# Moving 24 gathered rows and ten expert columns ahead of the gate stage's end, with scores one unit later

## The chip, the cores and the metric

One core of one Trainium2 chip runs the kernel. The metric is the device time of one execution in microseconds, lower is better. The kernel before took 2283.4 us (median of three runs, 2283.37 to 2287.0).

## The reference, cut to what matters

Two transformer blocks over 512 tokens of width 1024, in fp32. The change lies in the last layer, a retrieval of experts: each token scores 16 x 128 sub-keys, keeps 16 experts for each of 8 heads out of 16384, and adds up their outputs.

```python
def block(xb):
    q = (xb @ w_query).reshape(T, PEER_HEADS, 2, PEER_HALF)
    s = jnp.einsum('thpk,hpnk->thpn', q, sub_keys).astype(jnp.float32)
    top_s, top_i = lax.top_k(s, PEER_TOPK)
    ...
    best_s, best_pos = lax.top_k(cand_s.reshape(T, PEER_HEADS, PEER_TOPK * PEER_TOPK), PEER_TOPK)
    idx = jnp.take_along_axis(..., best_pos, axis=-1)
    gate = jax.nn.softmax(best_s, axis=-1)
    u = expert_u[idx]
    v = expert_v[idx]
    act = jax.nn.gelu(jnp.einsum('td,thkd->thk', xb, u).astype(jnp.float32), approximate=False)
    return jnp.einsum('thk,thkd->td', (gate * act).astype(xb.dtype), v)
```

## The kernel before

Tokens are four tiles of 128. The expert layer, `peer`, treats them in two ways.

**Tile 0 by rows.** `gather` (L1065) reads, for each of 128 expert slots, one row of u and later one row of v for every token, by an indirect DMA that the POOL queue issues (L1074, 512 KB each, 256 in all, four buffers `grow`). VectorE reduces a u row with the token's activations (L1077) or adds a v row into `acc0` (L1079). In the program these rows stand in `experts_out`, about two behind each column.

**Tiles 1 to 3 densely.** The 16384 experts are 128 columns of 128. For a column, `expert_in` (L1056) makes the hidden activations of the 384 tokens: `unit` (L189) loads 512 KB of weights into one of three `raw` buffers, ScalarE writes the high part `whi` (L200), VectorE or POOL the low part `wlo` (L201) into one of eight buffers of the pool `wsp`, TensorE does 24 matmuls of 384 tokens (L206 to L208), ScalarE the Gelu (L1062). An even column is made early and spilled to `actD` (64 of them, NSPILL); odd columns are made fresh in the last stage.

`peer` runs in four stages, whose instructions a planner orders on each engine by program order and modelled readiness; every engine then works its queue in order.
- **Scores** (`route`, L1095 to L1108): 16 units of the query; after each unit's projection ScalarE copies q, TensorE multiplies it with the sub-keys (L1103), and VectorE takes the top 16 (`top16`).
- **Top 16 of the pairs** (L1109 to L1158): VectorE alone, with TensorE on expert columns beside it.
- **Gates** (`gates_dense`, L1180): 96 blocks of four tokens. A block needs a tile A (the first index's one-hot times the gate) and a tile B (the second index's one-hot), then small matmuls (L1216) and a copy (L1218). Tile A is built by POOL in blocks 2 and 6 of eight (L1199), by ScalarE in 0 and 4 (L1203, L1204), by VectorE otherwise (L1210); B by VectorE (L1213, and L1206 where ScalarE built A). There are six buffers each. The blocks leave through `gst` to `gD` in memory. 24 steps of four blocks each.
- **Products with v** (`experts_out`, L1226): for each column, `parts` takes the activations (spilled, or fresh), loads the gates `gt` for eight columns at a time (L1247), multiplies (L1257), splits (L1261, L1262), loads v, and 18 matmuls of 512 follow (`prod`). Three columns (1, 3, 5) are made ahead of the first product.

`pace` (L1039) says how many columns are traced beside each stage: 3 and 2 beside the scores, 45 beside the top 16, 14 beside the gates. Their `wlo` is VectorE's work in the 45 and POOL's in the others.

## Time and profile before

| | |
|---|---|
| median of three runs | 2283.4 us |
| the profiled execution | 2284.21 us |
| its span | 2282.4 us |
| TensorE busy, share of the span | 96% |
| VectorE, ScalarE, POOL busy | 74%, 40%, 30% |
| mean granted TensorE clock | 0.986 |

The profile lists what each engine did and when, from the span's start. A busy share is an average over the whole span; the stages differ. In the views below a number such as `x118` counts instructions; a part in brackets or behind the bar says how long the engine sat idle and what ended that. `PEclk` is the share of full clock that TensorE was granted: 1.00 is 2.4 GHz, 0.50 is 1.2 GHz. The stages of `peer` lie at about 990 to 1140 us (scores), 1140 to 1319 (top 16), 1313 to 1462 (gates) and 1462 to 2282 (products).

### The profile page before, as it was taken

What the parts mean: (1) busy time and instruction counts of PE and PEld (TensorE: products, weight loads), DVE (VectorE), ACT (ScalarE), POOL (GpSimd) and SP (SyncE); (2) the same over time, 40 slices, a digit from 0 to 9 for tenths busy, and PEclk for the clock granted to TensorE, in tenths of its full rate; (3) what the DMA queues carried; (4) which work ended last, traced back from release to release, by engine and by line L of the source; (5) the groups of instructions that cost most, each with busy time, mean ns of one, the idle gap of its engine ahead of it and who ended that gap; (6) DMA issues with size and microseconds to landing.
All of it is one profiled execution on the core that took longest, in us unless ns stands there. A gap on an engine that the chain in (4) does not pass through costs nothing. (4 is left out here: it accounts for less than half of the span.)

```text
span 2282.4 us, 32112 instructions
## 1 busy us (share of the span) xinstructions
PE 2201.8 (96%) x11849; PEld 1952.1 (86%) x11849; DVE 1680.1 (74%) x3126; ACT 922.4 (40%) x1540; POOL 690.0 (30%) x558
## 2 busy tenths in 40 slices
PE   7998999999999999989999989889999999999997
PEld 6786878888889888877999989878888888888886
DVE  5347557888426478567799999678888787888888
ACT  4225444333325443342344468533333333333332
POOL 2223110000002223210000587533444444444445
PEclk9998999999999999999999999989999999999999
DMA  8324006767322221042355546799999999999996
GB/s 274 99 69 120 10 1 210 246 210 230 102 92 87 92 84 56 10 159 85 128 171 180 161 174 252 290 325 349 338 340 343 355 333 339 330 345 335 346 340 216
DMA packets 165645, 469.53 MB, mean 206 GB/s; under 512 B 18800, under 2 KB 62704, under 8 KB 165360
## 3 DMA queue, kind: packets, MB, share of 16 engines
q1 hardware_dynamic: 128624, 333.25, 42.7%
q0 software_dynamic: 36864, 134.23, 16.0%
q8 instruction: 93, 1.52, 0.3%
q14 instruction: 64, 0.52, 0.1%
HBM read 422.31 MB, written 39.85 MB: 202 GB/s over the span
## 5 line engine op out<-in xcount | busy, mean ns | idle before, releaser
L206 PE MATMUL b<-hh,wlo 128*128 128x384 f32 (+2 forms) x1872 | 655.5, 351 | 6.3 <-DVE wlo L201 3.1
L207 PE MATMUL b<-hl,whi 128*128 128x384 f32 (+2 forms) x1872 | 652.9, 349 | 3.3 <-DVE hl L288 3.2
L208 PE MATMUL b<-hh,whi 128*128 128x384 f32 (+2 forms) x1872 | 652.3, 349 | 0.0
L201 DVE TENSOR_TENSOR wlo<-raw,whi 128x1024 fp32r<-128x1024 f32 x375 | 455.3, 1222 | 201.4 <-ACT whi L200 195.4
L200 ACT ACTIVATE whi<-raw 128x1024 fp32r<-128x1024 f32 (+1 forms) x405 | 425.3, 1054 | 363.2 <-PE b L208 148.9
L206 PEld LDWEIGHTS b<-hh,wlo 128*128 128x128 f32 x1872 | 353.4, 189 | 34.2 <-DVE wlo L201 3.7
L207 PEld LDWEIGHTS b<-hl,whi 128*128 128x128 f32 x1872 | 354.2, 189 | 30.4 <-DVE hl L288 3.8
L208 PEld LDWEIGHTS b<-hh,whi 128*128 128x128 f32 x1872 | 353.9, 189 | 24.7
L206 PE MATMUL b<-whi,wl 128*128 128x512 f32 x768 | 299.9, 390 | 12.3 <-DVE wl L1262 12.3
L208 PE MATMUL b<-whi,wh 128*128 128x512 f32 x768 | 300.9, 392 | 0.0
L207 PE MATMUL b<-wlo,wh 128*128 128x512 f32 x768 | 300.8, 392 | 0.0
L201 POOL TENSOR_TENSOR wlo<-raw,whi 128x1024 fp32r<-128x1024 f32 x30 | 80.0, 2678 | 640.7 <-ACT whi L200 635.7
L1074 POOL DMA_INDIRECT grow<-in_p_ur_dram,eid x128 | 177.2, 1385 | 234.7 <-DVE gact L1077 166.9
L1074 POOL DMA_INDIRECT grow<-in_p_v_dram,eid x128 | 172.1, 1345 | 217.8 <-DVE acc L1079 132.8
L1062 ACT ACTIVATE act<-b 128x384 f32<-128x384 f32 x114 | 55.7, 492 | 382.4 <-PE b L208 301.4
L206 PE MATMUL b<-whi,hl 128*128 128x512 f32 (+1 forms) x464 | 178.9, 387 | 3.3 <-DVE hl L254 2.3
L206 PEld LDWEIGHTS b<-whi,wl 128*128 128x128 f32 x768 | 144.9, 189 | 41.4 <-DVE wl L1262 12.6
L208 PE MATMUL b<-whi,hh 128*128 128x512 f32 (+1 forms) x464 | 177.9, 384 | 0.0
L207 PE MATMUL b<-wlo,hh 128*128 128x512 f32 (+1 forms) x464 | 177.7, 383 | 0.0
L208 PEld LDWEIGHTS b<-whi,wh 128*128 128x128 f32 x768 | 144.7, 188 | 30.4
L207 PEld LDWEIGHTS b<-wlo,wh 128*128 128x128 f32 x768 | 144.8, 189 | 29.0
L1079 DVE SCALAR_TENSOR_TENSOR acc<-grow,gact,acc 128x1024 f32<-128x1024 f32 x127 | 162.7, 1281 | 3.4 <-DMA grow<-in_p_v_dram,eid 2.4
(296 smaller groups left out, 2953.6 us busy)
## 6 DMA issues: line engine op xcount, KB each, us to landing
raw<-in_p_u_dram SPq DMA_DIRECT2D x128, 512.0 KB
raw<-in_p_v_dram SPq DMA_DIRECT2D x128, 512.0 KB
raw<-in_w_adaT_dram SPq DMA_DIRECT2D x48, 512.0 KB
gD<-gst SPq DMA_DIRECT2D x48, 512.0 KB
gt<-gD SPq DMA_DIRECT2D x16, 1536.0 KB
raw<-in_w_up_dram SPq DMA_DIRECT2D x44, 512.0 KB
raw<-in_w_t_dram SPq DMA_DIRECT2D x32, 512.0 KB
acts<-actD SPq DMA_DIRECT2D x64, 192.0 KB
```

What stands on the lines that cost most here:

```text
L200: nc.scalar.activation(hi, raw, AF.Copy)
L201: (eng or nc.vector).tensor_tensor(lo, raw, hi.bitcast(F32), op=ALU.subtract)
L206: mm(out, al, bh, start=start, stop=False)
L207: mm(out, ah, bl, start=False, stop=False)
L208: mm(out, ah, bh, start=False, stop=stop)
L1062: self.nc.scalar.activation(act, ps, AF.Gelu)
L1074: nc.gpsimd.indirect_dma_start(out=g, out_offset=None, in_=rows[n], in_offset=bass.IndirectOffsetOnAxis(ap=self.eid[:, s:s + 1], axis=0))
L1079: nc.vector.scalar_tensor_tensor(self.acc0, g, act[:, s:s + 1], self.acc0, op0=ALU.mult, op1=ALU.add)
```

## The change

- **Columns**: 74 of 128 are spilled instead of 64; the 54 fresh ones are spread evenly (2, 4, 7, 9, 11, 14, 16, ...). `pace` becomes 3 and 2 beside the scores, 49 beside the top 16 (`wlo` on VectorE), 20 beside the gates (`wlo` on POOL). Six fresh columns instead of three are made ahead of the products.
- **Rows**: the first 24 gathered rows (16 of u, 8 of v) are traced one per step of the gate stage; `tc.issue_after` keeps their POOL instruction behind the last POOL instruction of the step's blocks and their VectorE instruction behind the last B. The other 232 stay in the last stage.
- **Scores**: the multiplication with the sub-keys of unit m stands behind the projection of unit m+1 and writes other banks (1 to 3 instead of 6 and 7).
- **Gates**: in blocks 0 and 4 ScalarE now multiplies the gate into A (four small Relu instead of one wide one, with a negated copy of the gates in `sel[3]`), and VectorE builds B with one wide comparison instead of four small ones. Buffers of A and B fall from six to four each, with four apart for spilled activations.
- **Buffers**: `wsp` has six buffers instead of eight in `peer`; in the last stage `raw` has five instead of three, and the activations have eight fixed tiles.

```diff
-NSPILL = 64
+NSPILL = 74
+NACT = 8
...
     def unit(self, src, eng=None):
-        raw = self.wraw.tile([128, 1024], F32, name="raw")[:, :src.shape[-1]]
+        self.turn = (self.turn + 1) % len(self.raws)
+        raw = self.raws[self.turn].tile([128, 1024], F32, name="raw")[:, :src.shape[-1]]
...
+            if n > 1:
+                wsp.close()
+                wsp = ctx.enter_context(ExitStack())
+                self.wsp = wsp.enter_context(tc.tile_pool(name=f"wsp{n}", bufs=8 if n == 2 else 6, reuse_waits="tile"))
...
+            g0 = [self.gather(P)]
+            fresh = [j for j in range(128) if (j + 1) * (128 - NSPILL) // 128 > j * (128 - NSPILL) // 128]
...
-                pace = [(1, 3), (15, 2), (32, 45), (24, 14)]
+                pace = [(1, 3, 0, nc.gpsimd), (16, 2, 0, nc.gpsimd), (32, 49, 0, nc.vector), (24, 20, 24, nc.gpsimd)]
...
+                        for _ in range(part(cols)):
+                            act = (self.gpool or Q).tile([128, NIN], F32, name="act", bufs=4)
+                            j = todo.pop(0)
+                            self.expert_in(act, psp, j, eng)
+                            nc.sync.dma_start(self.actD[self.slot[j]], act)
+                        if part(r0):
+                            with tc.issue_after(self.marks[0]), tc.issue_after(self.marks[1]):
+                                _advance(g0, part(r0))
...
-            for m in range(16):
...
+            for m in range(17):
+                if m < 16:
+                    w = self.unit(a["w_q"][m])
+                    ps = psp.tile([128, S], F32, name="t")
+                    self.proj_t(ps, w, self.hh, self.hl)
+                    qs[m] = R.tile([128, S], F32, name="q", bufs=2)
+                    nc.scalar.activation(qs[m], ps, AF.Copy)
+                if m:
+                    q = qs.pop(m - 1)
+                    ps = psp.tile([128, NT, 128], F32, name="g")
...
-                    A = G.tile([128, S], F32, name="ga", bufs=6).rearrange("p (a b) -> p a b", a=4)
+                    A = G.tile([128, S], F32, name="ga", bufs=4).rearrange("p (a b) -> p a b", a=4)
...
                         for i in range(4):
                             nc.scalar.activation(A[:, i], iota, AF.Abs, bias=ii[:, i:i + 1], scale=-1.0)
-                        nc.scalar.activation(A, A, AF.Relu, bias=self.ones, scale=-1.0)
                         for i in range(4):
-                            nc.vector.tensor_scalar(B[:, i], iota, jj[:, i:i + 1], gg[:, i:i + 1], op0=ALU.is_equal,
-                                                    op1=ALU.mult)
+                            nc.scalar.activation(A[:, i], A[:, i], AF.Relu, bias=gg[:, i:i + 1], scale=ng[:, i:i + 1])
                     else:
+                        eng = nc.gpsimd if t4 in GP else nc.vector
...
+                        if t4 in GP:
+                            self.marks[0] = e.ins
+                    e = nc.vector.tensor_tensor(B, iota[:, None, :].to_broadcast([128, 4, 128]),
+                                            jj[:, :, None].to_broadcast([128, 4, 128]), op=ALU.is_equal)
+                    self.marks[1] = e.ins
...
+            more = c0.enter_context(tc.tile_pool(name="wraw2", bufs=2, reuse_waits="tile"))
+            self.raws = self.raws * 3 + [more] * 2
...
-            early = {j: self.expert_in(T, psp.only("pre"), j, nc.vector) for j in (1, 3, 5)}
+            acts = [P.tile([128, n], F32, name=f"acts{i}") for i in range(NACT)]
+            free = list(range(NACT))
+            early = {}
+            for j in fresh[:6]:
+                early[j] = acts[free.pop(0)]
+                self.expert_in(early[j], psp.only("pre"), j, nc.vector)
...
-                goal = min(257, 257 * (j + 1) // GBY)
-                _advance(gather, goal - done)
+                goal = min(rest, rest * (j + 1) // GBY)
+                with tc.issue_after(self.marks[0]), tc.issue_after(self.marks[1]):
+                    _advance(gather, goal - done)
```

## Rows read from the trace of the kernel before

**Rows 1.** Windows: us, busy us (count) of PE, PEld, DVE, ACT, POOL; PEclk, DMA, GB/s.

```profile
1160.00:1180.00 20.00, 20.00 (x118) 20.00 (x117) 20.00 (x60) 9.64 (x13) 0.00 (x0) 1.00 0.47 156
990.00:1140.00 150.00, 143.23 (x741) 124.81 (x740) 102.97 (x524) 50.44 (x73) 4.80 (x2) 1.00 0.34 113
1312.70:1321.70 9.00, 0.82 (x4) 0.23 (x3) 8.93 (x13) 2.63 (x5) 6.16 (x5) 0.64 0.21 71
1321.70:1325.50 3.80, 3.80 (x18) 3.80 (x19) 3.80 (x13) 0.61 (x2) 1.66 (x2) 0.50 0.00 0
1490.70:1496.10 5.40, 5.38 (x13) 4.22 (x14) 4.13 (x8) 0.47 (x2) 2.26 (x3) 0.50 0.97 332
1496.10:2260.00 763.90, 763.90 (x3693) 673.71 (x3692) 623.35 (x806) 270.00 (x372) 341.43 (x248) 1.00 0.93 337
1319.00:1458.00 139.00, 136.23 (x1036) 135.21 (x1037) 138.51 (x368) 105.90 (x230) 116.85 (x96) 0.98 0.61 232
```

**Rows 2.** Waits of PE, 985 to 1500 us: us in total, times, longest.

```profile
PE b L206 <- DVE wl L1262: 12.3, 1, 12.3
PE b L1166 <- DVE si L1141: 6.1, 1, 6.1
PE b L1103 <- ACT q L1100: 5.7, 8, 0.7
PE b L206 <- DVE wlo L201: 2.8, 1, 2.8
```

**Rows 3.** Timelines of ACT, SP, DVE and PE from the last gates to the first product.

```profile
1461.70 0.60 ACT L1218 ACTIVATE gst<-b 128x512 f32<-128x512 f32 x1 [0.29 <-PE b L1216]
...
1471.67 0.38 SPq L1247 DMA_DIRECT2D gt<-gD  x1
...
1485.01 1.96 DVE L1257 TENSOR_TENSOR act<-act,gt 128x384 f32<-128x384 f32 x4 [9.93 <-DMA gt<-gD]
...
1490.72 0.79 PE L206 MATMUL b<-whi,wl 128*128 128x512 f32 x1 [12.26 <-DVE wl L1262]
```

**Rows 4.** Groups of PE by form, from 975 to 1478.5 us, then to 1312.9 us.

```profile
L208 PE MATMUL b<-hh,whi 128*128 128x384 f32 x544 | 184.2, 339 | 0.0
...
L208 PE MATMUL b<-hh,whi 128*128 128x384 f32 x424 | 142.9, 337 | 0.0
```

**Rows 5.** Groups of instructions in the gate stage, 1319 to 1458 us.

```profile
L1199 POOL TENSOR_SCALAR ga<-c_iota,sel,sel 128x128 f32<-128x128 f32 x92 | 107.0, 1174 | 22.1 <-PE b L1216 10.5 <-DVE gb L1213 5.0 <-ACT gst L1218 3.7
...
L1213 DVE TENSOR_TENSOR gb<-c_iota,sel 128x512 f32<-128x512 f32 x72 | 50.5, 720 | 0.0
...
L1206 DVE TENSOR_SCALAR gb<-c_iota,sel,sel 128x128 f32<-128x128 f32 x96 | 27.7, 362 | 0.0
...
L201 POOL TENSOR_TENSOR wlo<-raw,whi 128x1024 fp32r<-128x1024 f32 x4 | 10.0, 2500 | 0.0
L201 DVE TENSOR_TENSOR wlo<-raw,whi 128x1024 fp32r<-128x1024 f32 x8 | 9.7, 1212 | 0.0
```

**Rows 6.** Timelines of DVE and POOL around one split on POOL.

```profile
1322.13 1.11 DVE L1210 TENSOR_SCALAR ga<-c_iota,sel,sel 128x128 f32<-128x128 f32 x4
...
1327.19 3.28 DVE L1210 TENSOR_SCALAR ga<-c_iota,sel,sel 128x128 f32<-128x128 f32 x4
...
1327.99 2.39 POOL L201 TENSOR_TENSOR wlo<-raw,whi 128x1024 fp32r<-128x1024 f32 x1
```

**Rows 7.** Timeline of POOL: its first splits for the gate stage's columns.

```profile
1272.45 11.55 POOL L201 TENSOR_TENSOR wlo<-raw,whi 128x1024 fp32r<-128x1024 f32 x3 [206.83 <-ACT whi L200]
```

**Rows 8.** Costliest groups of the whole page: the rows' POOL and VectorE instructions.

```profile
L1074 POOL DMA_INDIRECT grow<-in_p_ur_dram,eid x128 | 177.2, 1385 | 234.7 <-DVE gact L1077 166.9 <-DVE acc L1079 57.3 <-issue 8.8
...
L1079 DVE SCALAR_TENSOR_TENSOR acc<-grow,gact,acc 128x1024 f32<-128x1024 f32 x127 | 162.7, 1281 | 3.4 <-DMA grow<-in_p_v_dram,eid 2.4
```

**Rows 9.** POOL's instructions of L1199: ns min/median/max, first and last start.

```profile
L1199 POOL TENSOR_SCALAR ga<-c_iota,sel,sel x96: 784/1064/2444, 1313.1 to 1457.0; 128x128 f32<-128x128 f32 x96
```

**Rows 10.** Timeline of POOL: one row's indirect DMA.

```profile
1461.27 0.94 POOL L1074 DMA_INDIRECT grow<-in_p_ur_dram,eid  x1 [0.30 <-issue]
```

More of the change, by code (lines that the diff above doesn't have):

```diff
@@ L26 @@
 BIG = -1e30
-NSPILL = 64
+NSPILL = 74
+NIN = 384
 AHEAD = 2
@@ L1033, in peer @@
             self.gate0 = P.tile([128, 128], F32, name="gate0")
+            self.grows = c0.enter_context(tc.tile_pool(name="grows", bufs=GROWS, reuse_waits="tile"))
+            g0 = [self.gather(P)]
+            fresh = [j for j in range(128) if (j + 1) * (128 - NSPILL) // 128 > j * (128 - NSPILL) // 128]
+            self.slot = {j: k for k, j in enumerate(j for j in range(128) if j not in fresh)}
             with ExitStack() as c1:
@@ L1052, in peer, with expert_in @@
+                assert not todo
                 while work:
                     _advance(work)
[L1054 to L1057 removed]
+            self.experts_out(fresh, g0, sum(p[2] for p in pace))
+    def expert_in(self, act, psp, j, eng):
         w = self.unit(self.a["p_u"][j], eng=eng)
[L1059 to L1061 removed]
+        ps = psp.tile([128, S], F32, name="u")[:, :NIN]
+        self.proj_t(ps, w, self.hh, self.hl, slice(S - NIN, S))
@@ L1062, in expert_in, with row @@
         self.nc.scalar.activation(act, ps, AF.Gelu)
-        return act
+    def row(self, n, eid):
+        g = self.grows.tile([128, D], F32, name="grow")
+        self.nc.gpsimd.indirect_dma_start(out=g, out_offset=None, in_=self.a[n].rearrange("j i d -> (j i) d"),
+                                          in_offset=bass.IndirectOffsetOnAxis(ap=eid, axis=0))
+        return g
     def gather(self, P):
-        tc, nc, a = self.tc, self.nc, self.a
-        rows = {n: a[n].rearrange("j i d -> (j i) d") for n in ("p_ur", "p_v")}
+        nc = self.nc
@@ L1072, in gather @@
                 for s in range(16 * h, 16 * h + 16):
-                    g = P.tile([128, D], F32, name="grow", bufs=GROWS)
-                    nc.gpsimd.indirect_dma_start(out=g, out_offset=None, in_=rows[n],
-                                                 in_offset=bass.IndirectOffsetOnAxis(ap=self.eid[:, s:s + 1], axis=0))
+                    g = self.row(n, self.eid[:, s:s + 1])
                     if n == "p_ur":
```

99 lines of the change are left out of this document (40 added, 59 removed).

## The prediction, made before the changed kernel was seen

> **What bounds the kernel now.** I read the windows by stage first, then what TensorE waited for, then the timelines at its gaps, and last the groups of the gate stage. From 1496 to 2260 us TensorE is busy without a break: 763.90 of 763.90 us [rows 1]. The change neither adds nor removes a matmul of a column or of a product: 128 columns and 128 products stay. So the time can move only with TensorE's idle time and its clock, and `peer` has 34.7 us of both up to the first product:
> - 6.8 us beside the scores (143.23 busy of 150), where each of eight multiplications with the sub-keys stands behind the copy of q [rows 1, 2];
> - 8.2 us at 1312.7 to 1321.7, ended by VectorE's last index work, and 1.9 us more because the following 3.80 busy us run at a granted clock of 0.50, that is 1.2 GHz, after that idle time [rows 1, 2];
> - 2.8 us for a weight split and 12.3 us for the first product [rows 2], then 2.7 us from 5.38 busy us at 0.50 [rows 1], again after idle time.
>
> The 12.3 us are the end of a chain: the last gates are copied at 1461.7, `gt` is issued at 1471.7, VectorE starts on it at 1485.0, the first product runs at 1490.7 [rows 3]. That is 29.0 us from the end of the gates, and TensorE had columns for only part of it.
>
> **One sum for the whole change.** A column is 24 matmuls; 118 of them take 20 us, so 0.1695 us each and 4.07 us a column [rows 1]. Before, 68 columns (544 matmuls of L208 at 8 each) are done ahead of the first product [rows 4]: 64 spilled, 1, 3, 5, and column 7. After it will be 74 + 6 = 80. The twelve that are gone from behind the first product save 12 x 4.07 = 48.8 us there, and the slow clock's 2.7 us go if the gap is short. Against that the first product comes later. If the gates end at G, it comes at G + 29.0, so
>
> change = (G - 1461.7) - 48.8 - 2.7 = G - 1513.2.
>
> Everything hangs on G, that is, on which engine paces the gate stage. No engine was far from it: VectorE was busy 138.51 of 139 us, TensorE 136.23, POOL 116.85 [rows 1].
>
> **G by TensorE.** The moved scores take 6.8 us away: one unit's projection now lies between the copy and its user, and the copy is under a microsecond long. Four more columns beside the top 16 (16.3 us) cover the gap of 8.2 + 1.9. Ten more columns ahead of G cost 40.7: 1461.7 - 16.9 + 40.7 = 1485.5.
>
> **G by VectorE.** Its stage began at 1319. It starts 6.8 earlier, pays four more splits (4 x 1.21 = 4.8 [rows 5]), and gains from this: while POOL does one split of 2.39 us, four of VectorE's instructions take 3.28 instead of 1.11 us [rows 6], so a split on POOL costs VectorE 2.17 us. Ten of the 14 POOL splits fell before 1319 (four are left after it [rows 5]). POOL's first, for column 51, starts at 1272.45 [rows 7], when column 43 is through, as the eight buffers say; with six it waits for column 49 of column 55, and about five fall before the stage. Five fewer are 10.9 us: 1319 - 6.8 + 4.8 - 10.9 = 1306.1. In the stage: 138.5 less 4 x 2.17 and less 9.7 for eight splits is 120.1; four comparisons become one in 24 blocks, 27.7 against 24 x 0.70 = 16.8, so -10.9 [rows 5]; 24 rows at 1.28 add 30.7 [rows 8]; six early splits 7.3; fifteen POOL splits 32.6. That is 179.8, an end at 1485.9 and, with the 3.7 us that lay between VectorE's end and the last copy, G = 1489.6.
>
> **G by POOL.** A blocks start at 1313.1 before [rows 9]; by the same three terms they start at 1300.2. By lookahead three splits are done by then (column 53 ended at 1312.7, 424 / 8 [rows 4], so column 49 will end at 1312.7 - 4 x 4.07 - 6.8 = 1289.6). POOL then has 17 splits at 2.50 (42.5), 96 A instructions at 1.174 (112.7) [rows 5] and 24 row DMAs. A row is 0.94 us and 0.30 to the next [rows 10], 29.8 in all; in the last stage it is 1.385 [rows 8], which is the upper end (+10 with its gaps). An A instruction is 0.784 at its shortest [rows 9], so 37.4 us of the 112.7 are stretch, and I put it down to VectorE's two-input instructions beside it, 50.5 + 9.7 us in 139, 43% of the stage [rows 5]. After, these are 67.3 + 30.7 + 7.3 = 105.3 in 195, or 54%, so the stretch becomes 47, +10. Sum 42.5 + 122.7 + 29.8 = 195.0, an end at 1495.2, and with the 3.9 us from POOL's last A (1457.0 + 0.8) to the last copy G = 1499.1. Without stretch it is 1489, with slow rows too 1509.
>
> POOL ends last: **G = 1499, change -14.1 us**. Against the profiled execution (2284.2 with a span of 2282.4) that is 2270.1; the median of the runs is 0.8 lower, so **2269 us**. TensorE then idles about 14 us inside the gate stage and 29.0 - 6 x 4.07 = 4.6 before the products; the old gaps are filled, and half of their worth is given back here.
>
> **The other edits.** ScalarE gets three more small instructions in 24 blocks, 72 at no more than the 0.60 us of a wide copy [rows 3], 43 us on 105.9 of 139 [rows 1]; in a stage of 195 us it still has room, so nothing. The rows' DMAs go on POOL's queue beside SP's: 24 x 0.52 MB, six column loads and their spills add about 94 GB/s to 232, 326 where the last stage runs at 337 [rows 1]; nothing, but no room is left. A row's VectorE instruction waits for its landing, and the next blocks' A and B, then TensorE's small matmuls, queue behind it. From 1458 on such waits were 3.4 us in 127 [rows 8]; at worst one is a third of the 13.3 us that `gt` took for three times the bytes [rows 3], 4.4 us, paid once rather than 24 times, since VectorE then trails POOL by it. I take 0. The smaller buffer counts and the reopened pool have no row of their own; the nearest wait is the 2.8 us for a split [rows 2], and I take 0. In the last stage VectorE and POOL lose work and TensorE was not waiting, so no gain there.
>
> **A rule beside this.** VectorE and POOL exclude each other, in part for A and wholly for a split [rows 5, 6, 9]. The Trainium skill (SBUF — State Buffer, Who interferes with whom) says that a VectorE instruction with two SBUF inputs and a GpSimd instruction that reads SBUF block each other fully, for a whole instruction. Taken so, all 105.3 us would add to POOL's 147.6 of bare work, G would be 1557 and the kernel 44 us slower, an estimate by that page. The trace agrees for the split and not for A: 37.4 us of stretch stand beside 60.2 us of such work.
>
> **The rivals.**
> 1. *TensorE or VectorE paces the gates.* The stretch doesn't grow, or the planner leaves rows behind the gates, so that the change doesn't place them as it says. G is 1486 to 1492: -27 to -21, 2256 to 2262. For it: POOL idled 22.1 us in the stage [rows 5], so it was not the bound. All gaps filled would be -34.7, 2249.
> 2. *The gain is just given back.* G is 1507 to 1518, 2277 to 2288, near the bound of no change. For it: three queues near full, each in order, four buffers instead of six between them.
> 3. *Slower: POOL shuts.* The A instructions and the two-input work exclude each other more. Of the 105.3 us, 61.5 may fall on POOL before the sum turns (1513.2 - 3.9 - 1300.2 - 147.6), a share of 0.58; I assume 0.45, and the old stage shows 37.4 / 60.2 = 0.62 of it. At a share of 0.8, G is 1536 and the time 2306. Against it: POOL was busy with A in 77% of the old stage and will be in 63%, so fewer of them meet.
> 4. *The last stage starves.* A spilled column takes 18 products' time and wants v, `gt`, activations and two rows, about 1.9 MB in 4.1 us, 470 GB/s where 337 are moved [rows 1]; about 20 pairs of such columns now stand together where before none did. Five `raw` buffers should cover a pair's lack of 1 MB. If not, 1 us a pair makes +20 on the forecast, 2289.
>
> **How the numbers follow.** Forecast 0.40 (2262 to 2277), rival 1 0.22, rival 2 0.17, rival 3 0.16, rival 4 0.05. A measurement of this kernel tells about 0.2% from no change, that is 2278.8 to 2288.0. Faster: the forecast, rival 1 and a little of rival 2, 0.65; slower: rivals 3, 4 and a tail of 2, 0.20; same 0.15. The range runs from all gaps filled to where rival 3 begins, 2249 to 2290, and leaves out most of rival 3 and half of 4. Cases of both signs hold weight; the forecast's own range is 2262 to 2277.
>
> **What the profile after would show.** TensorE's waits for the copy of q and the gap at 1312 gone; no idle time ended by L1141; POOL's A and splits end last in the gate stage, at a mean of about 1.28 us for an A; the last copy of gates near 1499 and the first product near 1528; a clock of 1.00 behind it; the last stage again without a wait of TensorE. I am wrong if G falls under 1492 or over 1507, if the 29.0 us of the chain change, or if TensorE waits after the first product.

## The result, and the profile after the change

| | before | after |
|---|---|---|
| median | 2283.4 us | 2307.1 us (2306.46 to 2313.79, five runs) |
| ratio to before | | 1.0108, 95% interval 1.0091 to 1.0124 |
| the profiled execution, its span | 2284.21, 2282.4 us | 2308.17, 2306.4 us |
| mean granted TensorE clock | 0.986 | 0.983 |

The kernel became 1.1% slower; the forecast was 0.6% faster. Lines have moved: L203 and L204 are the two parts of a split, L209 to L211 the long matmuls, L1081 a row's DMA, L1094 and L1096 its VectorE instruction (u, v), L1228 and L1232 tiles A and B, L1236 the gate matmuls, L1272 the load of `gt`, L1286 its multiplication.

Windows of the changed kernel (us, busy us and count of PE, PEld, DVE, ACT, POOL; PEclk, DMA, GB/s); the last gate matmul ends at 1520.1, the first product starts at 1565.0:

```profile
640.00:960.00 320.00, 312.72 (x1760) 272.95 (x1759) 181.78 (x291) 129.88 (x215) 79.82 (x79) 0.99 0.22 72
960.00:1150.00 190.00, 184.55 (x968) 165.78 (x967) 151.53 (x655) 75.69 (x118) 14.26 (x9) 0.98 0.34 114
1150.00:1300.60 150.60, 150.60 (x872) 150.46 (x871) 145.52 (x285) 62.82 (x88) 3.58 (x2) 1.00 0.52 173
1300.60:1519.95 219.35, 200.07 (x1384) 195.48 (x1383) 169.23 (x331) 146.97 (x341) 196.44 (x139) 0.98 0.69 236
1519.95:1565.00 45.05, 22.86 (x122) 22.40 (x121) 26.72 (x32) 11.07 (x17) 15.91 (x14) 0.77 0.99 371
1565.00:2290.00 725.00, 725.00 (x3457) 633.12 (x3456) 593.83 (x765) 256.17 (x355) 286.39 (x220) 1.00 0.92 333
```

The products still run without a break, as in [rows 1], and TensorE had all the top 16 filled. It stands idle in two places: 19.3 us among the gates, which now take 219 us, and 22.2 us between them and the first product. That stretch is 45 us long; it was 29.0 [rows 3].

Groups of the gate stage, 1300.6 to 1519.95 us (the answer to [rows 5]):

```profile
L1228 POOL TENSOR_SCALAR ga<-c_iota,sel,sel 128x128 f32<-128x128 f32 x96 | 121.0, 1267 | 18.1 <-PE b L1236 17.9
L204 POOL TENSOR_TENSOR wlo<-raw,whi 128x1024 fp32r<-128x1024 f32 x19 | 47.4, 2511 | 0.8 <-ACT whi L203 0.4
L1081 POOL DMA_INDIRECT grow<-in_p_ur_dram,eid x16 | 18.9, 1182 | 2.6 <-issue 2.6
L1081 POOL DMA_INDIRECT grow<-in_p_v_dram,eid x8 | 9.3, 1165 | 1.3 <-issue 1.3
...
L1094 DVE CUSTOM_DVE_ANT_0 grow<-grow,h 128x1024 f32<-128x1024 f32 x16 | 30.8, 1922 | 29.8 <-DMA grow<-in_p_ur_dram,eid 29.8
L1096 DVE SCALAR_TENSOR_TENSOR acc<-grow,gact,acc 128x1024 f32<-128x1024 f32 x6 | 7.7, 1287 | 8.9 <-DMA grow<-in_p_v_dram,eid 8.9
```

VectorE waits 38.7 us for rows to land, and 4.0 us more for the first v row: 42.7 us in 14 waits. POOL ends last, as forecast, but not without rest: it waits 17.9 us for TensorE to give tile A back. Timelines of POOL, VectorE and TensorE around one row show how one wait leads to the other:

```profile
1332.47 1.03 POOL L1081 DMA_INDIRECT grow<-in_p_ur_dram,eid  x1 [0.17 <-issue]
...
1341.38 4.65 POOL L204 TENSOR_TENSOR wlo<-raw,whi 128x1024 fp32r<-128x1024 f32 x2
1354.08 4.68 POOL L1228 TENSOR_SCALAR ga<-c_iota,sel,sel 128x128 f32<-128x128 f32 x4 [8.04 <-PE b L1236]
...
1339.22 1.23 DVE L1094 CUSTOM_DVE_ANT_0 grow<-grow,h 128x1024 f32<-128x1024 f32 x1 [5.21 <-DMA grow<-in_p_ur_dram,eid]
1340.37 6.27 DVE L1228 TENSOR_SCALAR ga<-c_iota,sel,sel 128x128 f32<-128x128 f32 x4
1346.56 1.28 DVE L1232 TENSOR_TENSOR gb<-c_iota,sel 128x512 f32<-128x512 f32 x2
...
1347.39 2.05 PE L1236 MATMUL b<-gb,ga 128*128 128x128 f32 x8 [5.46 <-DVE gb L1232]
```

VectorE waits 5.21 us for a row that POOL asked for 6.75 us before; beside two splits on POOL its four instructions for an A then take 6.27 us (1.11 at 1350.00). So TensorE waits 5.46 us for a B, and POOL 8.04 us until TensorE gives an A back. A second row, asked for at 1375.18, shows the split's part by itself:

```profile
1375.18 1.04 POOL L1081 DMA_INDIRECT grow<-in_p_ur_dram,eid  x1 [0.16 <-issue]
...
1382.39 4.72 POOL L204 TENSOR_TENSOR wlo<-raw,whi 128x1024 fp32r<-128x1024 f32 x2
...
1380.00 0.68 DVE L1232 TENSOR_TENSOR gb<-c_iota,sel 128x512 f32<-128x512 f32 x1
1383.02 5.19 DVE L1094 CUSTOM_DVE_ANT_0 grow<-grow,h 128x1024 f32<-128x1024 f32 x1 [2.34 <-DMA grow<-in_p_ur_dram,eid]
```

VectorE has done its last B and waits 2.34 us for that row; when it has it, two splits on POOL stretch its 1.2 us to 5.19. From 1380.68 to 1388.14, 7.5 us, it builds no gate tile.

Timelines of SP, ACT, DVE and PE from the last gates to the first product (the answer to [rows 3]):

```profile
1468.66 0.43 SPq L195 DMA_DIRECT2D raw<-in_p_v_dram  x1
...
1509.81 14.20 SPq L1243 DMA_DIRECT2D gD<-gst  x8
1534.65 0.81 SPq L195 DMA_DIRECT2D raw<-in_p_u_dram  x2
...
1536.38 0.38 SPq L1272 DMA_DIRECT2D gt<-gD  x1
...
1540.17 1.06 ACT L203 ACTIVATE whi<-raw 128x1024 fp32r<-128x1024 f32 x1 [14.41 <-DMA raw<-in_p_u_dram]
...
1544.26 1.28 DVE L1096 SCALAR_TENSOR_TENSOR acc<-grow,gact,acc 128x1024 f32<-128x1024 f32 x1 [4.97 <-DMA grow<-in_p_v_dram,eid]
1545.46 5.76 DVE L204 TENSOR_TENSOR wlo<-raw,whi 128x1024 fp32r<-128x1024 f32 x5
1553.53 1.96 DVE L1286 TENSOR_TENSOR acts<-acts,gt 128x384 f32<-128x384 f32 x4 [2.32 <-DMA gt<-gD]
...
1546.73 0.69 PE L209 MATMUL b<-hh,wlo 128*128 128x384 f32 x1 [21.50 <-DVE wlo L204]
```

For 66 us SP asks for no weights. The next load goes into one of the two new `raw` buffers, whose memory the gates held, and waits until their last transfers are through (SP stands 10.5 us at it); `gt` stands behind it. Four of the six early columns are done only behind that wait, and on VectorE their splits queue behind v rows that have yet to land.

**A ledger of TensorE's losses.** Its matmuls are the same in all kernels here, so its idle time (a window's length less PE's busy time) plus half of its busy time at a granted clock of 0.50 says when its last matmul comes, to within some 7 us by which the busy time that is left differs (2181.5 to 2188.5 us); "tail" is what lies behind that. Up to 640 us the same code loses 26 to 33 us from run to run; that is left out. Each row is of the profiled execution, which for one_wsp is the fastest of four (2292.5 us). The runs below are the experiments.

| us lost | 640 to 960 | 960 to 1150 | to the last gates | to the first product | products | tail |
|---|---|---|---|---|---|---|
| before | 3.8 | 13.1 | 10.8 | 15.1 | 2.6 | 13.1 |
| **after** | 8.7 | 8.1 | 23.4 | 23.9 | 0 | 15.9 |
| scores_only | 3.7 | 7.4 | 1.1 | 11.1 | 2.1 | 23.5 |
| scores_ga_232 | 3.7 | 7.7 | 1.2 | 10.7 | 2.2 | 8.0 |
| scores_rows | 3.7 | 7.8 | 13.9 | 16.3 | 2.2 | 8.2 |
| rows_back | 8.7 | 8.0 | 0.6 | 18.8 | 0 | 59.8 |
| rows_out | 8.7 | 8.0 | 0.6 | 24.2 | 0 | 13.8 |
| cols64 | 10.4 | 7.3 | 36.0 | 29.3 | 0.6 | 8.1 |
| cols64_r8 | 3.7 | 8.1 | 27.3 | 25.5 | 1.2 | 9.7 |
| row_lag | 8.9 | 8.1 | 15.7 | 25.1 | 0 | 15.5 |
| one_wsp | 3.7 | 8.3 | 20.7 | 21.3 | 0 | 14.6 |
| raw_first | 9.0 | 8.4 | 26.0 | 23.1 | 0 | 15.8 |
| all3 | 3.7 | 8.2 | 14.5 | 23.2 | 0 | 14.7 |
| rows_hold | 9.0 | 8.5 | 22.2 | 17.9 | 0 | 25.1 |
| raws3 | 9.0 | 8.5 | 30.2 | 15.2 | 11.7 | 8.3 |
| raws3_fixed | 3.7 | 8.2 | 19.0 | 16.1 | 18.4 | 8.3 |
| late_raws | 9.0 | 8.3 | 31.5 | 14.1 | 7.2 | 11.5 |
| late_raws_fixed | 3.7 | 8.1 | 17.7 | 15.0 | 7.0 | 11.3 |

### The profile page after: what moved, and what is told of

It is laid out like the page before. It is cut to its first block, busy times and chain, and to the rows that moved or that the text cites. A ratio compares the mean times of both kernels' runs of the same rounds, so it can differ in the third digit from the quotient of the medians.

```text
span 2306.4 us, 32191 instructions
## 1 busy us (share of the span) xinstructions
PE 2206.7 (96%) x11849; PEld 1958.5 (85%) x11849; DVE 1675.3 (73%) x3048; ACT 939.7 (41%) x1615; POOL 688.8 (30%) x564
## 3 DMA queue, kind: packets, MB, share of 16 engines
q0 software_dynamic: 36864, 134.23, 16.3%
## 5 line engine op out<-in xcount | busy, mean ns | idle before, releaser
L209 PE MATMUL b<-hh,wlo 128*128 128x384 f32 (+2 forms) x1872 | 660.0, 353 | 32.5 <-DVE wlo L204 25.8
L211 PE MATMUL b<-hh,whi 128*128 128x384 f32 (+2 forms) x1872 | 657.0, 351 | 0.0
L204 DVE TENSOR_TENSOR wlo<-raw,whi 128x1024 fp32r<-128x1024 f32 x369 | 451.6, 1228 | 232.3 <-ACT whi L203 229.6
L203 ACT ACTIVATE whi<-raw 128x1024 fp32r<-128x1024 f32 (+1 forms) x405 | 425.2, 1054 | 446.2 <-PE b L211 317.8
L209 PEld LDWEIGHTS b<-hh,wlo 128*128 128x128 f32 x1872 | 356.2, 191 | 60.1 <-DVE wlo L204 26.6
L211 PEld LDWEIGHTS b<-hh,whi 128*128 128x128 f32 x1872 | 355.8, 190 | 24.3
L211 PE MATMUL b<-whi,wh 128*128 128x512 f32 x768 | 299.6, 390 | 0.0
L209 PE MATMUL b<-whi,wl 128*128 128x512 f32 x768 | 298.0, 389 | 0.0
L1081 POOL DMA_INDIRECT grow<-in_p_ur_dram,eid x128 | 163.8, 1280 | 243.7 <-DVE gact L1094 163.7
L1081 POOL DMA_INDIRECT grow<-in_p_v_dram,eid x128 | 165.6, 1294 | 221.0 <-DVE acc L1096 151.8
L204 POOL TENSOR_TENSOR wlo<-raw,whi 128x1024 fp32r<-128x1024 f32 x36 | 92.4, 2579 | 327.7 <-ACT whi L203 327.3
L1094 DVE CUSTOM_DVE_ANT_0 grow<-grow,h 128x1024 f32<-128x1024 f32 x128 | 165.9, 1307 | 31.3 <-DMA grow<-in_p_ur_dram,eid 31.3
L209 PE MATMUL b<-whi,hl 128*128 128x512 f32 (+1 forms) x464 | 179.5, 388 | 3.1 <-DVE hl L257 2.1
L1096 DVE SCALAR_TENSOR_TENSOR acc<-grow,gact,acc 128x1024 f32<-128x1024 f32 x127 | 162.9, 1283 | 26.7 <-DMA grow<-in_p_v_dram,eid 25.6
L211 PE MATMUL b<-whi,hh 128*128 128x512 f32 (+1 forms) x464 | 178.3, 385 | 0.0
L211 PEld LDWEIGHTS b<-whi,wh 128*128 128x128 f32 x768 | 144.1, 188 | 30.1
L210 PEld LDWEIGHTS b<-wlo,wh 128*128 128x128 f32 x768 | 144.1, 188 | 28.9
L209 PEld LDWEIGHTS b<-whi,wl 128*128 128x128 f32 x768 | 144.2, 188 | 28.8
```

What stands on the lines that cost most here:

```text
L203: nc.scalar.activation(hi, raw, AF.Copy)
L204: (eng or nc.vector).tensor_tensor(lo, raw, hi.bitcast(F32), op=ALU.subtract)
L209: mm(out, al, bh, start=start, stop=False)
L210: mm(out, ah, bl, start=False, stop=False)
L211: mm(out, ah, bh, start=False, stop=stop)
L1081: self.nc.gpsimd.indirect_dma_start(out=g, out_offset=None, in_=self.a[n].rearrange("j i d -> (j i) d"), in_offset=bass.IndirectOffsetOnAx ...
```

## The experiments

The ratios are to runs of the kernel before on the same chip.

### What was lost, undone one by one

**rows_back**: the 24 rows return to the last stage.
```diff
-                pace = [..., (24, 20, 24, nc.gpsimd)]
+                pace = [..., (24, 20, 0, nc.gpsimd)]
```


> The changed kernel without its rows among the gates: all 256 rows are gathered in the last stage. Theory (rows cost the gate stage more than POOL's 28 us, since VectorE waits for them): the gate stage shrinks from 219 to about 190 us or less, the last stage keeps its pace since TensorE limits it, and the time falls by 25 us or more to 2282 or less. Rival (the last stage is limited by its transfers, so that 24 rows more, 12.6 MB at 337 GB/s or 37 us, come back there): TensorE waits in the last stage and the time stays between 2298 and 2315.

2321.1 us, 1.0152 (1.0135 to 1.0169): slower than the change. Windows of this run, gates, products and behind them:

```profile
1299.80:1493.40 193.60, 193.00 (x1384) 191.81 (x1383) 137.58 (x291) 146.54 (x340) 159.00 (x117) 1.00 0.56 205
1533.60:2258.00 724.40, 724.40 (x3453) 632.58 (x3452) 595.20 (x769) 256.56 (x356) 298.35 (x225) 1.00 0.94 337
2258.00:2295.00 37.00, 1.11 (x5) 0.57 (x4) 29.27 (x38) 0.21 (x1) 21.16 (x20) 0.56 0.82 273
```

Without rows TensorE is full among the gates, and the last matmul comes 31 us sooner, at 2259.1. But the rows then go on without it for 42 us. The theory was right on the gates and wrong on the time; the rows do come back in the last stage, as the rival had it, but behind TensorE's end and not as waits of TensorE, and they cost more than its 2315. From 1650 to 2200 us they pass at 14 to 17 per 50 us here and in the changed kernel, though TensorE is 31 us further here: a second queue beside the products that sets the end when it is longer. Where it waits, it waits for VectorE: from 1600 to 2200 us POOL stands 343.5 us until VectorE gives a row's buffer back; what VectorE's order would allow beyond that was not tried. With the products nearly through, from 2250 to 2300 us, 26 rows pass.

**rows_out**: the 24 rows are left out altogether.
```diff
+                    if s < (16 if n == "p_ur" else 8):
+                        continue
```


> The changed kernel with the 24 rows of the gate stage left out altogether (16 of u and 8 of v are not read and not used); the other 232 rows stay in the last stage. Against the run with all 256 rows in the last stage it shows what 24 rows cost there, and against the changed kernel what they cost among the gates. Theory (with 232 rows TensorE sets the last stage, with 256 the rows do): the gates end at 1493 as in that run, the first product comes near 1533, TensorE works 725 us on end and a tail of 17 us follows: 2275 to 2279. Rival (the rows or the DMA engines set the last stage in both): the gates' end plus the 786 us that lay behind it in the changed kernel, or more, 2280 to 2290, with waits of TensorE or a tail over 20 us.

2278.9 us, 0.9977 (0.9965 to 0.9988), gates to 1493.4, a tail of 13.8: the theory held. So 24 rows cost 28 us among the gates (2307.1) and 42 in the last stage (2321.1); by the ratios, as the three ran on different chips, 30 and 40. And a change whose rows are free is still only 4.5 us faster than before.

**cols64**: the columns return.
```diff
-NSPILL = 74
+NSPILL = 64
-                pace = [..., (32, 49, 0, nc.vector), (24, 20, 24, nc.gpsimd)]
+                pace = [..., (32, 45, 0, nc.vector), (24, 14, 24, nc.gpsimd)]
...
-            for j in fresh[:6]:
+            for j in fresh[:3]:
```


> The changed kernel with the columns put back alone: 64 spilled, 45 beside the top 16 and 14 beside the gates, three instead of six made ahead of the products; the 24 rows, the buffers, the scores and the gate blocks stay as changed. Theory (among the gates the 24 rows and the 20 columns' splits compete for POOL's and VectorE's queues; six POOL splits of 2.51 us fewer, 15 us, nearly end TensorE's 18 us of idle time there, and the three columns ahead of the products have their weights loaded already, so that the chain is about 30 us again): 2285 to 2293. Rival (the rows alone make the idle time, with any number of columns): gates longer than TensorE's work by 15 us or more, 2298 to 2306.

2319.2 us, 1.0151 (1.0133 to 1.0169). Theory and rival both fell by their times; of the rival it came true that the gates are longer than TensorE's work by 15 us or more (28.1). The gate stage and TensorE's waits from its start to the first product:

```profile
1296.00:1494.70 198.70, 170.60 (x1174) 164.22 (x1172) 167.52 (x333) 134.66 (x322) 171.34 (x131) 0.95 0.65 229
```
```profile
PE b L209 <- DVE wlo L204: 24.0, 1, 24.0
PE b L1236 <- DVE gb L1232: 20.6, 10, 7.0
PE b L1236 <- POOL ga L1228: 5.7, 10, 1.0
```

Ten columns less are 40.7 us of TensorE's work, yet the gates end only 25 us sooner (1494.9), and TensorE stands idle 28.1 of the stage's 198.7 us. So the gates with 24 rows among them take near 200 us even with 14 columns, and of the 40.7 us that the change put ahead of their end some 15 filled time in which TensorE would have stood idle. Three early columns instead of six make the way to the products 7 us shorter (38.0), but TensorE loses 5.4 us more in it.

**row_lag**: a row's DMA goes out one step ahead of its VectorE instruction.
```diff
+            g = nxt
...
+                nxt = self.row(jobs[k + 1][0], self.eid[:, ...])
```


> The changed kernel with one edit: a row's indirect DMA is traced one step ahead of VectorE's instruction that uses it, so that VectorE meets a row that was issued some 9 us before. Theory (VectorE's waits for the rows' landing stretch the gate stage): the 43 us that VectorE waited for rows in that stage go to under 10, the stage of 219 us becomes about 200, the time falls by 15 to 20 us to about 2289. Rival (POOL paces the stage, busy 196 of 219 us, as my forecast had it): the waits go but the stage keeps 212 us or more, and the time falls by less than 7 us, 2300 or more.

2298.0 us, 1.0061 (1.0044 to 1.0078), between theory and rival. VectorE's waits in the gate stage (L1231, L1235 and L1239 are this kernel's A, B and gate matmul):

```profile
DVE ga L1231 <- PE b L1239: 15.2, 13, 3.6
DVE gb L1235 <- PE b L1239: 13.7, 2, 12.4
DVE grow L1096 <- DMA grow<-in_p_ur_dram,eid: 4.6, 2, 2.4
DVE acc L1101 <- DMA grow<-in_p_v_dram,eid: 2.7, 1, 2.7
...
DVE acc L1098 <- DMA grow<-in_p_v_dram,eid: 0.4, 1, 0.4
```

The 42.7 us for landings are 7.7, and the loss among the gates falls by 8, the time by 9. The wait for a landing was real and paid in 14 of 24 steps. Two thirds of the loss stay, 15.7 us, and they are POOL's for the most part: TensorE's waits for a B fall from 12.2 to 3.3 us, those for POOL's A stay (5.8, now 8.0), POOL is busy 195.0 of 211.6 us, and VectorE now waits 28.9 us for TensorE.

**one_wsp**: the weight buffers `wsp` are one pool of six for the whole kernel and one of two that is given up, instead of a pool closed and opened at each border.
```diff
+        wspa = ctx.enter_context(tc.tile_pool(name="wspa", bufs=6, reuse_waits="tile"))
-                self.wsp = wsp.enter_context(tc.tile_pool(name=f"wsp{n}", bufs=8 if n == 2 else 6, ...))
```


> The changed kernel with one edit: six of the eight buffers of split weights stay one pool from the start to the end; only a pool of two is closed at the stage borders. In the changed kernel the first column starts at 985.1 us instead of 972.7, behind waits of 4.0 and 5.5 us for a split at the two borders. Theory (a reopened pool makes the first splits of a stage wait for the old stage's last matmuls): the first column comes back to about 973 us and the time falls by about 12 us to 2295. Rival (a later stage that is paced by VectorE or POOL absorbs it): the start comes back but the time falls by less than 4 us.

2301.9 us, 1.0079 (1.0056 to 1.0103), runs from 2292.5 to 2306.4: between theory and rival, and too wide to tell the time from the changed kernel's. TensorE's waits at the borders in the changed kernel, 640 to 990 us:

```profile
PE b L209 <- POOL wlo L204: 5.5, 1, 5.5
PE b L209 <- DVE wlo L204: 4.0, 1, 4.0
```

Both are gone here, and the first column of `peer` starts at 970 us; in the nine kernels with reopened pools it starts at 979 to 986, in before at 973. In the ledger it is 5 us; in the stretch behind, a new wait of 4.3 us for `hl` (L292 of this kernel) takes the second one's place.

**raw_first**: the new `raw` buffers are placed ahead of the tiles of the last stage.
```diff
+            more = c0.enter_context(tc.tile_pool(name="wraw2", ...))
             T = c0.enter_context(tc.tile_pool(name="eow", ...))
-            more = c0.enter_context(tc.tile_pool(name="wraw2", ...))
```


> The changed kernel with one edit: in the last stage the pool of the two extra raw buffers is opened ahead of the pool of gates, so that these buffers no longer lie in the memory of gst. In the changed kernel SP issues no weight load between 1469 and 1535 us, and the load at 1534.65 waits for the last gD transfers. Theory (the buffers' memory holds the queue up): the 21.5 us wait of TensorE for a split disappears, the first product comes about 29 us after the last gates instead of 45, and the time falls by about 16 us to 2291. Rival (the transfers themselves are the limit there, the DMA share is 0.97 to 1.06 from 1525 to 1565): only their order changes, at most 4 us, 2303 or more.

2304.8 us, 1.0089 (1.0072 to 1.0106): the rival's number. The waiting load went at 1521.1, 3 us behind the gates instead of 15, but its data were there only 12.6 us later, beside the rows, and VectorE's split of it stood behind eight rows, at 1541.4. The way to the products stayed at 44 us: lifting the queue's wait alone uncovers the next one.

### The way from the gates to the products

**rows_hold**: no row's VectorE instruction ahead of the second column's split.
```diff
+                if j < AHEAD:
+                    self.marks[1] = e.ins
```


> The changed kernel, with one difference: the rows left for the last stage have their VectorE instruction ordered behind the split of the second column's activations, so that no more than four rows are read between the last gates and the first product. Theory (the rows behind the gates hold VectorE's splits and load the DMA engines, so the chain of 45.2 us from the gates' end to the first product shortens): chain 30 to 36 us, time 2292 to 2299. Rival (the last stage ends when the bytes are through, whatever starts first): the first product comes sooner, but the rows end later and the time stays at 2305 to 2312.

2308.2 us, 1.0111 (1.0092 to 1.0130). The way fell to 38.9 us, the tail grew by 9: the rival. The rows end last, and what was held back at the start comes off again at the end.

**raws3** (three `raw` buffers to the end) and **late_raws** (five from the second column's weights on):
```diff
-            more = c0.enter_context(tc.tile_pool(name="wraw2", ...))
-            self.raws = self.raws * 3 + [more] * 2
```
```diff
-            self.raws = self.raws * 3 + [more] * 2
...
             ready = [parts(j) for j in range(AHEAD)]
+            self.raws = self.raws * 3 + [more] * 2
```


> The changed kernel with three raw buffers to the end, as before, instead of five from the last stage on. In the changed kernel a weight load into one of the two new buffers waits at the head of SP's queue until the gate stage's memory is free, and the first gates' load stands behind it: the gates end at 1519.8, the next load goes at 1534.7, the first product at 1565.0. Theory (the new buffers make the chain long): loads go on during the gates, the chain falls from 45.2 to 26 to 33 us, and the time to 2290 to 2298. Rival A (the chain is the DMA engines' load, rows included, and not the order of the queue): chain 38 us or more, time 2302 or more. Rival B (the chain falls but the rows then end last): chain under 33 us, last row still near 2281, time 2302 to 2307.

> The changed kernel with the two further raw buffers taken into the turn only after the second column's weights of the products are asked for: three buffers up to there, five behind. With three to the end TensorE lost 15.2 us from the last gates to the first product instead of 23.9, and 11.7 us in the last stage instead of none. Theory (both are had: the order of SP's queue made the chain long, five buffers keep the last stage fed): the chain's loss 13 to 17 us, the last stage's under 2, time 2294 to 2302. Rival (the gates' end moves later by what the chain gains, as with three buffers, where it went from 219 to 230 us behind the stage's start): 2304 to 2309.

2306.9 us, 1.0100 (1.0077 to 1.0123), and 2303.9, 1.0093 (1.0076 to 1.0110). The way is 32.2 and 31.2 us long, so the two buffers did make it long. Little was won: in late_raws the gates take 231 us instead of 219, as the rival had it. raws3 has the way and the time of its rival B, but not its reason: its last row is read at 2255.4 and the tail is 8.3, so TensorE ends last, and the gain went to longer gates (231 us) and to the products. Among the gates the early columns' splits now fall on VectorE, in late_raws seven instead of two:

```profile
1296.90:1528.40 231.50, 207.74 (x1408) 203.36 (x1407) 178.56 (x336) 152.89 (x347) 204.88 (x143) 0.96 0.70 241
1528.40:1559.70 31.30, 18.90 (x98) 18.13 (x96) 16.71 (x18) 7.57 (x15) 9.32 (x8) 0.85 1.01 383
```
```profile
L204 DVE TENSOR_TENSOR wlo<-raw,whi 128x1024 fp32r<-128x1024 f32 x7 | 8.6, 1225 | 0.0
```

With three buffers to the end the products lose 11.7 us, in late_raws 7.2, in the changed kernel none.

**all3** is row_lag, one_wsp and raw_first together; **raws3_fixed** and **late_raws_fixed** are row_lag and one_wsp with raws3 or with late_raws. Their edits are those above.

> The changed kernel with three edits together: the weight buffers not reopened at the borders, each row's DMA issued one step ahead of its VectorE instruction, and the two further raw buffers placed ahead of the tiles of the last stage. Theory (the three losses lie one behind the other and add): alone they moved the span from 2306.4 to 2290.6, 2296.3 and 2303.0, that is -15.8, -10.1 and -3.4; together 2277 (2273 to 2282). Rival (the gate stage is one ring of four buffers among POOL, VectorE and TensorE, and what one edit frees another engine takes back): 2286 or more.

> The changed kernel with three raw buffers to the end, each row's DMA issued one step ahead, and the weight buffers not reopened. Theory (the three losses add): the run with the other two edits had a span of 2290.2 and a chain of 44.5 us; 12 to 17 us less, 2274 to 2279, still no faster than the kernel before with the scores alone (2271). Rival (the rows or the loads of the last stage set the end): 2285 or more.

> The same with each row's DMA one step ahead and the weight buffers not reopened, that is the changed kernel with all three losses undone. Theory (they add): the run with the last two alone gave 2292; 6 to 10 us less, 2282 to 2286, no better than the kernel before, since 24 rows among the gates still cost TensorE about 15 us there. Rival (rows or loads set the end): 2290 or more.

2292.2 us, 1.0033 (1.0020 to 1.0045); 2299.4, 1.0074 (1.0055 to 1.0092); 2289.4, 1.0037 (1.0021 to 1.0052). All three miss their theories, by 3 to 20 us; the first two lie where their rivals had them, the third between. Each loss can be undone where it stands, but the stretches to the last gates, to the first product and of the products trade with one another: 37.7 us in sum in all3, 39.7 in late_raws_fixed, 53.5 in raws3_fixed, 47.3 in the changed kernel. None is as fast as before.

### Parts alone on the kernel before

**scores_only**, and **scores_ga** with the changed gate blocks as well:
```diff
-            for m in range(16):
+            for m in range(17):
...
+                if m:
+                    q = qs.pop(m - 1)
```
```diff
-                        nc.scalar.activation(A, A, AF.Relu, bias=self.ones, scale=-1.0)
+                            nc.scalar.activation(A[:, i], A[:, i], AF.Relu, bias=gg[:, i:i + 1], scale=ng[:, i:i + 1])
```


> The kernel before with only the multiplication with the sub-keys moved one unit later and to the other banks. Theory (the 6.8 us beside the scores are TensorE's and come off the path): no wait for q, the end 5 to 7 us sooner, 2277 to 2280. Rival (VectorE's top 16 sets when the gates start, and TensorE only waits longer there): 2282 to 2286, with the gap at the border to the gates wider than 8.2 us.

> The kernel before with the scores one unit later and the changed gate blocks (ScalarE multiplies the gate into tile A, one wide comparison for tile B), with the old buffers. Theory (in the gate stage of the run with the scores alone VectorE was busy 119 of 135 us and TensorE 132, so VectorE's 11 us less change nothing): within 2 us of that run, 2268 to 2274. Rival (VectorE's order holds the gates' start, and 11 us less bring them sooner): 2262 to 2267.

2271.2 us, 0.9944 (0.9927 to 0.9960), and 2270.1, 0.9944 (0.9927 to 0.9962): both beat the kernel before and the changed one. The scores alone give twice the theory, the gate blocks nothing, as expected. Windows of scores_only to the last gates and to the first product:

```profile
1150.00:1441.60 291.60, 290.51 (x1956) 289.92 (x1954) 282.20 (x621) 174.47 (x330) 150.73 (x112) 1.00 0.59 205
1441.60:1467.10 25.50, 16.14 (x84) 15.50 (x82) 7.86 (x12) 7.04 (x12) 3.38 (x4) 0.89 0.98 344
```

The gap of 8.2 us at 1312 [rows 1] is gone with nothing put into it: VectorE gets its scores sooner, and the first A block starts at 1288.5 instead of 1313.1 [rows 9]. TensorE's last matmul comes 24 us sooner (2245.3 against 2269.4), the end only 13.6. The chain that ended last in scores_ga shows who took the rest:

```profile
2229.40 5.76 DMA grow<-in_p_v_dram,eid
2235.25 1.30 DVE acc L1079
...
2249.82 1.21 DVE acc L1079
2251.16 2.48 POOL acc L1278 x2
...
2264.01 1.30 DVEq L1364
```

**scores_ga_232**: scores_ga with 24 rows left out, as in rows_out.

> The kernel before with the scores one unit later and the changed gate blocks, and 24 rows (16 of u, 8 of v) left out: not read and not used. With all 256 rows TensorE's last matmul came at 2244.5 and the end at 2268.3. Theory (the rows set that end once TensorE is sooner): without 24 of them TensorE sets it, 13 to 16 us behind its last matmul, 2257 to 2262. Rival (the end is TensorE's and the long tail only the work behind it): 2266 to 2271.

2254.5 us, 0.9888 (0.9866 to 0.9910), somewhat past the theory. TensorE's last matmul stays at 2244.0 and the tail falls from 23.5 to 8.0: the rows had set the end, by 15 us. Beside rows_out (2278.9, with the same 232 rows) it also prices the columns and buffers without any rows among the gates: 24 us slower (20 by the ratios, as the chips differ). The ledger has 5 at the border, 13.5 on the way to the products and 6 in the tail; rows_out also lost 6.5 us more up to 640 us.

**scores_rows** puts eight rows of u among the gates of scores_only, read one step ahead; **cols64_r8** is cols64 with eight rows, row_lag and one_wsp.
```diff
+                        if n_ == 3 and (i + 1) * NROW // steps > i * NROW // steps:
...
+                                _advance(g0)
...
-                    B = G.tile([128, S], F32, name="gb", bufs=6)...
+                    B = G.tile([128, S], F32, name="gb", bufs=4)...
```


> The kernel before with the scores one unit later, and eight rows of u among the gates, each read one step ahead into two buffers of the gate stage (tile B has four buffers instead of six, tile A and the spilled activations five instead of six). With the scores alone TensorE's last matmul came at 2244.9 and the end 24 us behind it, at 2268.8, since the rows ended last. Theory (the rows set that end, and eight of them at 3.2 us each lie ahead now): TensorE sets the end again, 14 to 17 us behind its last matmul, 2259 to 2266. Rival (what eight rows cost among the gates is what they return): 2268 to 2275.

> The same with 64 columns, eight rows instead of 24 among the gates (one in every third step, all of u), each row's DMA issued one step ahead, and the weight buffers not reopened. Theory (few rows, read ahead, hide among the gates, and eight out of the last stage are enough for TensorE to set the end): TensorE idle under 12 us from 1280 us to the end, 2262 to 2270. Rival (the smaller buffer counts and the gate blocks themselves cost TensorE time): 2275 or more.

2277.5 us, 0.9973 (0.9961 to 0.9986), and 2300.7, 1.0072 (1.0052 to 1.0093): the rivals, and in scores_rows somewhat worse than the rival had it. There the tail falls from 23.5 to 8.2 as meant, but TensorE's last matmul comes 23 us later (2268.3 against 2245.3). TensorE loses 12.8 us more to the last gates and 5.3 more on the way to the products. The gate stage up to the last gate matmul:

```profile
1290.00:1461.20 171.20, 157.28 (x1149) 152.45 (x1148) 158.26 (x376) 113.29 (x239) 139.45 (x111) 1.00 0.64 231
```

In scores_only the stage takes 150.8 us. VectorE's eight rows are 10.7 us of its 158, and it waits 9.6 us for tiles that TensorE still holds, where in scores_only it waited for none. How much of the 20 us is the rows and how much the smaller buffers was not tried apart.

**scores_ga_110** spreads the rows over 110 columns instead of 120 (`GBY`).

> The kernel before with the scores one unit later and the changed gate blocks, and the rows of the last stage spread over 110 columns instead of 120. Without the last edit TensorE's last matmul came at 2244.5 and the end 23.8 us later, at 2268.3, because the rows ended last; 14 to 17 us lie behind the last matmul where TensorE ends last. Theory (the rows' order sets that end, and the DMA engines have a little room): the rows end 10 us sooner, 2259 to 2264. Rival (the last stage's DMA engines are full, and rows taken sooner make TensorE wait): 2268 to 2275 with waits of TensorE among the products.

2269.1 us, 0.9945 (0.9926 to 0.9964): no change to scores_ga, and no test. The planner put the rows almost where they had been (SP's queue is the same, 27 of POOL's 929 instructions stand in another place), so that this is nearly scores_ga measured twice.

## Why the prediction was wrong

**TensorE paces, and nothing else bounds the end: half right.** All differences are TensorE's idle time and clock, as the ledger shows. But the rows are a second queue that ends close to it already in before (last row read at 2263.7, TensorE's last matmul at 2269.4; a tail of 13.1 where 8 is possible). "In the last stage VectorE and POOL lose work and TensorE was not waiting, so no gain there" failed: rows_back, with 24 rows more in the last stage, is 14 us slower although its gates end 26 us sooner, and scores_only left 10 us of TensorE's gain to the rows.

**Twelve columns, 48.8 us, and the slow clock's 2.7: right.** From the first product to the end it was 791.7 us and is 741.4, that is 50.3 less.

**The scores, 6.8 us: near in size, but half of the effect was missed.** The waits for q (5.7 us) went, and the stretch gained 5.0 (5.7 in scores_only). The prediction let four more columns cover the gap of 8.2 + 1.9; the scores alone close it.

**G by POOL, 1499.1: 21 us short.** Its parts held: A blocks from 1300.6 (forecast 1300.2), an A at 1.267 us (1.28), so that A's stretch was 46.4 us (47). There were 19 splits in the stage, not 17 (+4.9), and a row took 1.34 us with its issue (1.24, +1.0 for the 23 ahead of its last A). The rest is POOL's 18.9 us of idle time, which the sum didn't have, less some 2 us at the end. The prediction's 326 GB/s there added a rate over some 180 us to one over 139; measured were 236 over 219 us. The start was right by luck: the columns came 12 us later (the border), VectorE's top 16 sooner (the scores).

**"Paid once rather than 24 times ... I take 0": the step that failed among the gates.** The rows that VectorE waited for came 4.2 to 9.7 us after POOL's instruction began, so that 4.4 us "at worst" was near the best case, and VectorE caught up with POOL again in most steps. The row's DMA was held behind POOL's last A of a step and its VectorE instruction behind the last B; that four buffers kept VectorE from trailing POOL is likely, but no run with 24 rows had more. It paid 14 times, 42.7 us; reading a row one step ahead took 35 of them and 9 us of time off, and left TensorE a loss of 15.7 us there, near the 14 that the prediction had. 23 rows took VectorE 41 us in the stage, where the prediction had 30.7 for 24: three u rows beside splits on POOL took 4.3 to 5.2 us each, the other 13 1.2 to 1.4.

**The chain, 29.0 us, taken as fixed: the larger failure.** It took 44.9, and TensorE lost 23.9 us in it where the prediction had 4.6. "The smaller buffer counts and the reopened pool have no row of their own ... I take 0": five `raw` buffers put weight loads and `gt` behind the gates' memory (with three the stretch is 32 us long), and six columns ahead didn't fill it, as four of them wait for weights themselves. The reopened pools cost another 5 us of TensorE's time. Beside that, the DMA engines are busy without rest in that stretch already before (a share of 1.01 at 353 GB/s from 1461.6 to 1490.7, 0.99 at 371 after): lifting the queue's wait alone, in raw_first, won 1 us of the way.

**In sum.** Against before the ledger has +12.6 among the gates, +8.8 to the first product, +4.9 at the border, +2.8 in the tail, +3.4 of run-to-run loss up to 640 us, -5.0 beside the scores and -2.6 behind the first product: +24.9 us, and the spans differ by 24.0. The forecast, put in these terms, was +3, -10.5, 0, 0, 0, -6.8 and -2.6; that is -17 where its own sum has -14, which takes the gaps a little otherwise.

**The rivals.** The time was that of rival 3 (2306), its mechanism was not: A's share of stretch was 46.4 us beside 107 us of VectorE's two-input work (B 65.6, rows 38.5, splits 2.5), 0.43 where the forecast had 0.45 and rival 3 0.8. Only 66 of the 107 us ran beside an A. Where they met, A lost most of the time (46.4 of 66 us; 51 A with 0.4 us or more of it beside them took 1.64 us on average, 16 with next to none 0.80) and VectorE nothing (a B 0.69 us beside an A, 0.68 without). The Trainium skill (SBUF — State Buffer, Who interferes with whom) has a VectorE instruction with two SBUF inputs and a GpSimd instruction that reads SBUF contend, and calls the port pair between them an exclusive lock. The trace agrees for a split on POOL and a u row on VectorE (1383.02 above), and for A in part, as only A waited; the prediction's 1557 let all of VectorE's work fall on POOL, which the Trainium skill does not say. Rivals 1 and 4 did not happen; the products don't starve (725 of 725 us). Rival 2's three queues in order with four buffers are nearest to what the gates did, but it had the loss end at 1518 and the chain as before. The range to 2290 had no room for a landing paid in many steps or for a longer chain.

## What to carry to other kernels

A wait for data that has just been asked for can be paid at use after use (14 of 24 here) unless the order of both queues lets the asker run ahead; ask a step earlier, and count what the reader's queue holds behind it. A buffer cut from memory that another stage still holds is a wait in the queue that fills it, and so for everything behind it there; price each change of a pool like an instruction. Before moving work ahead of the bounding engine, look for the queue that ends second: here the scores' small move brought TensorE's end 24 us sooner and the kernel's only 13.6, since the rows then ended last.

## What the runs showed of the hardware

- A row of 512 KB by indirect DMA was there 4.2 us after POOL's instruction began at best, 9.7 at worst, with the DMA engines busy 0.69 of the stage. The Trainium skill (DMA: Bandwidth & Descriptors, Anatomy of one DMA) gives a fit by which a DMA on the POOL path takes 2.0 us plus its bytes over 436 GB/s, 3.2 us for this size, an estimate. The shortest is 1 us over that, about the length of POOL's instruction; the longest is three times it.
- Two splits on POOL (4.72 us) stretched one VectorE instruction with two inputs from 1.2 to 5.19 us. The mean of 16 such instructions among the gates was 1.92 us, with three of them beside splits; in the last stage it is 1.22. An A on POOL beside such work took 1.64 us instead of 0.80 and did not stretch it.
- In the last stage the DMA engines move 333 to 337 GB/s at 0.92 to 0.94 in before, in the changed kernel and in rows_back. The rows keep to 14 to 17 per 50 us from 1700 to 2150 us, with 232 of them (rows_out) or 256; POOL waits more than half of that time for VectorE to give row buffers back.
